# hi and lo of the attention stage's weight tiles from casting and adding DMAs, in a hybrid decoder block

## The chip, the cores and the metric

One core of one Trainium2 chip runs the whole kernel. The metric is the device time of one execution in microseconds; times shown are medians of several runs. The engines are TensorE (PE in the profile, its weight loads PEld), VectorE (DVE), ScalarE (ACT), GpSimd (POOL) and SyncE (SP), which issues DMAs.

## The reference

One decoder layer on 512 tokens of width 1024, in float32. The first half mixes tokens: a combined projection gives queries, three pairs of keys and values, gates, and the inputs of a short convolution.

```python
h = rms_norm(x, norm_mix_pre[l])
u = h @ w_in[l]
q, k_c, v_c, k_s, v_s, k_w, v_w, gl, b_g, c_g, x_t = jnp.split(u, split_points(), axis=-1)
o_nsa = nsa_attention(...)            # compressed, selected and window branch, gated
o_conv = short_conv_mixer(b_g, c_g, x_t, conv_mix_w[l])
y = jnp.concatenate([o_nsa, o_conv], axis=-1) @ w_out[l]
x = x + rms_norm(y, norm_mix_post[l])
h = rms_norm(x, norm_ffn_pre[l])
gu = causal_dwconv(h @ w_ffn_up[l], ffn_conv_w[l])
g, up = jnp.split(gu, 2, axis=-1)
y = (gelu(g) * up) @ w_ffn_down[l]
x = x + rms_norm(y, norm_ffn_post[l])
```

The compressed branch first runs its keys and values, in blocks of 32 tokens, through a small two-layer network (`compress_kv`); its first layer has 2048 x 256 weights for keys and as many for values.

## The kernel before

TensorE multiplies in the type float32r. To keep float32's accuracy every operand is kept as two float32r tiles: hi, the value rounded to 12 significant bits, and lo, the exact rest. A product is three passes, hi x hi, hi x lo and lo x hi (`mm3`, L166 to L169).

The dense weights come as tiles of 128 x 1024 through one `Stream` object, `W`, in the order of their use. `_load` (L68) takes one of three raw buffers and loads 512 KB by a DMA on SP (L72). `_split` (L75) takes one of four buffers of the ring, which holds hi and lo side by side; ScalarE copies the raw tile into hi (L84), and VectorE subtracts hi from the raw tile into lo (L85). For the tiles named in `pool_lo`, the eight of the compression's first layer, GpSimd does the subtraction. `next` hands out a tile and has `ahead` split two and load three more tiles further on.

The tiles in order are: v0 to v2 (values and gates), k0, k1 and c0 (keys of two branches, keys to compress), q0, q1, c1, q2, then with q3 the compression's first layer in eight tiles (`c1_0` to `c1_7`, in the profile `raw_c` and `w_c`) and for each of the four convolution channel tiles a gate g, an input x and an output gate b (`tg`, `tx`, `tb`); after that the output projection's eight (o4 to o7, o0 to o3), 44 of the MLP's first product and 22 of its second.

The start of the kernel, up to L357, runs in the order in which it is written. Behind that a scheduler orders each engine's instructions by their priority and by the time at which it expects their inputs, so TensorE's projection products (`filler`, L535) and the attention's pieces are interleaved. `fill` says how many steps of the projections go between the pieces. The order of the steps is a string: two tiles of the compression are used for one projection tile until all eight are done.

```python
ORDER = ("c1 q2:4 h0 q2:4 h1 q3:4 h2 q3:4 h3 g0:4 h4 g0:4 h5 x0:4 h6 x0:4 h7 s b0 "
         "g1 x1 b1 g2 x2 b2 g3 x3 b3")
```

Here hN is a tile of the compression's first layer (`hidden_steps`, eight products at L441), s its second layer, and a number behind a colon counts steps of three products. The attention goes through four query tiles and two groups of heads in parts. Each part takes logits (L593), adds the bias and finds the row minimum on VectorE (L597), exponentials on ScalarE (L599), scaling by the gate and the sum, for one of four heads on GpSimd (L611) and for three on ScalarE (L613), transposes on TensorE (L622), splits the result into hi and lo (L131, L132) and multiplies it by the values (L630, L631). VectorE also places the values to compress in blocks (L417), and GpSimd takes part in the convolution (L505, L507, L511).

Of the kernel before, what the change touches and what calls it, by code (L numbers as in the profile page):

```python
"""Hybrid decoder block (NSA heads + short convolution, then a gated conv MLP) on one core.

Float32 products run as three float32r passes over operands split exactly into
hi + lo (12 + 12 significant bits): hi*hi + hi*lo + lo*hi.  The attention logits
and the P.V products keep all four parts.

With these shapes N_SEL covers every key block (n_sel = SEQ / L_SLC) and WINDOW =
SEQ, so the selected and the sliding branch both see exactly the causal keys: top-k
only permutes the blocks, and softmax does not depend on their order.
"""  # L10
# [11 lines left out]
F32 = mybir.dt.float32  # L22
# [8 lines left out]
NT = S // P          # token tiles  # L31
KT = D // P          # contraction tiles of the model width
# [9 lines left out]
# the projections and the first layer of the compression as they fill the gaps of the attention:  # L42
# values to compress c1, queries q, hidden layer h, second layer s, then gate g, input x, output gate b
# [3 lines left out]
T_TILES = 20         # kc vc ks kw q0-3 then (c x b) x 4  # L47
WARM = 8             # products on zeros while the first loads are under way


def f32(ap):
    return ap.bitcast(F32)


class Stream:
    """The dense weights in the order of their use: loaded some tiles ahead, split fewer ahead."""

    def __init__(self, tc, nc, raw, ring, items, loads=3, splits=2):
        self.tc, self.nc, self.raw, self.ring, self.items = tc, nc, raw, ring, items
        self.loads, self.splits = loads, splits  # L60
        self.raws, self.tiles = [], []
        self.at = 0
        self.early = False     # whether the splits go before what was emitted shortly before them
        self.pool_lo = set()  # tiles whose lo part GpSimd makes
        self.pieces = {}     # tiles that are split in pieces of so many columns
        self.other = {}      # tiles that go to another pool than the ring

    def _load(self):  # L68
        n = len(self.raws)
        src, cols, name = self.items[n][:3]  # L70
        t = self.raw.tile([P, 1024], F32, tag="raw", name=f"raw_{name}")
        self.nc.sync.dma_start(t[:, :cols], src)  # L72
        self.raws.append(t)

    def _split(self):  # L75
        n = len(self.tiles)
        _, cols, name = self.items[n][:3]
        pool, tag, bufs = self.other.get(name, (self.ring, "ring", None))
        t = pool.tile([P, 2, 1024], F32R, tag=tag, bufs=bufs, name=f"w_{name}")
        eng = self.nc.gpsimd if name in self.pool_lo else self.nc.vector  # L80
        step = self.pieces.get(name, cols)
        for c in range(0, cols, step):
            cs = slice(c, c + step)
            self.nc.scalar.activation(t[:, 0, cs], self.raws[n][:, cs], AF.Copy)  # L84
            eng.tensor_tensor(t[:, 1, cs], self.raws[n][:, cs], f32(t[:, 0, cs]), op=ALU.subtract)  # L85
        self.tiles.append(t)

    def ahead(self, splits, loads):
        last = len(self.items)
        while len(self.tiles) < min(self.at + splits, last):  # L90
            while len(self.raws) <= len(self.tiles):
                self._load()
            with self.tc.high_priority(30) if self.early else nullcontext():
                self._split()
        while len(self.raws) < min(self.at + loads, last):
            self._load()

# [10 lines left out]
def block_kernel(ctx: ExitStack, tc: tile.TileContext, a, out):  # L108
# [20 lines left out]
    def split(hi, lo, src):  # L129
        """hi = src rounded to 12 significant bits, lo = src - hi (exact)."""  # L130
        act(hi, src, AF.Copy)  # L131
        nc.vector.tensor_tensor(lo, src, f32(hi), op=ALU.subtract)  # L132

    VK = [0, 2, 5, KT]       # the k tiles of the value columns, as they share a tile of the ring
# [29 lines left out]
    W.pool_lo |= {f"c1_{c}" for c in range(8)}  # L164
# [28 lines left out]
    # the tensor engine's clock comes up while the first loads are under way  # L193
# [6 lines left out]
    # bias tables: U[p, h, u] = -(bias of distance p + 384 - u), +BIG where it is negative  # L200
    # row r of vrows is the whole of vd; reading with a pitch one short shifts it by r
# [6 lines left out]
    def load(what):  # L208
        """A name of LOADS: w the next weights, g the gains, b and v the bias (its table, then its vector),
        s rows of shifted bias, T columns and x rows of the input."""  # L210
        if what == "w":
            W.ahead(0, len(W.raws) + 1)
        elif what == "g":
            nc.sync.dma_start(gT, a["g_mix_pre"])
        elif what == "b":
            nc.sync.dma_start(oh[:NB, :S], a["onehot"])
            nc.sync.dma_start(relT, a["relT"])
        elif what == "v":
            nc.sync.dma_start(vd[:, :S], vec[:NH, :S])
            nc.sync.dma_start(vd[:, S:], vbig)  # L220
        elif what[0] == "s":
            n = int(what[1])
            nc.sync.dma_start(vrows[n], bass.AP(tensor=vd.tensor, offset=vd.offset + n * 4 * 640,
                                                ap=[[0, P], [1, 4 * 640]]))
        elif what[0] == "T":
            k = int(what[1])
            nc.sync.dma_start(xT[:, k, :], a["xT"][k * P:(k + 1) * P, :])
        else:
            t = int(what[1])
            nc.sync.dma_start(xt[:, t, :], a["x"][t * P:(t + 1) * P, :])  # L230
# [17 lines left out]
    def rstd_of(ss, name):  # L248
        """1 / rms of a row from the two halves of its mean square."""
        r = const.tile([P, 1], F32, tag="rstd", bufs=4, name=name)  # L250
        nc.gpsimd.tensor_scalar(r, ss[:, 0:1], ss[:, 1:2], EPS, op0=ALU.add, op1=ALU.add)  # L251
        nc.gpsimd.tensor_tensor(r, r, mhalf, op=ALU.pow)
        return r
# [17 lines left out]
    # The mean square of a row divides what comes out of the products, not what goes in.  # L271
    R = const.tile([P, 2, NT], F32, name="R")        # 1 / rms and its negative, by token
    Rb = ph1.tile([P, S], F32, name="Rb")            # the same, by token along the row
# [114 lines left out]
    # queries, scaled by -1/8; even heads keep hi in the low half, odd heads in the high half  # L388
# [14 lines left out]
    # X[(l parity, d), l // 2, k/v, hi/lo, (group, block)] = kv + pe, the blocks padded to 32  # L403
# [25 lines left out]
    def hidden_steps(c):  # L429
        """First layer of the compression; rows 0-63 from X hi, rows 64-127 from X lo."""  # L430
# [3 lines left out]
        for l in range(2):  # L434
            l2 = 2 * c + l
            for kv in range(2):
                xs = X[:, l2, kv].rearrange("p s g n -> p (s g n)")
                for s in range(2):
                    cc = slice(l * 512 + kv * 256, l * 512 + kv * 256 + 256)
                    # one group over the bank: its first product opens it  # L440
                    MM(phs[0][:, kv * 256:kv * 256 + 256], xs, w[:, s, cc],  # L441
                       start=l2 == 0 and kv == 0 and s == 0, stop=l2 == 15 and kv == 1 and s == 1)
            yield

    def second_layer():
        w2 = ph1.tile([P, 2, 2, HD], F32, tag="gz", bufs=1, name="w2")     # (half, k/v)
# [127 lines left out]
    class Part:  # L574
        """Four heads of a group on a tile of queries: one branch, or both for the first tile."""
# [76 lines left out]
    def finish(o, i, g):  # L652
        # rows 0-63: V hi . P, rows 64-127: V lo . P
# [23 lines left out]
    for n, (i, g, bs) in enumerate(parts):  # L677
# [6 lines left out]
        # the share that goes between this part's pieces  # L684
# [45 lines left out]
    def token_major(w_tiles, ys, acts, on_half, on_tile, order):  # L730
        """The last products of a streamed contraction, one token tile after another."""
# [14 lines left out]
    with tc.tile_pool(name="ph2", bufs=1, reuse_waits="tile") as ph2:  # L746
# [49 lines left out]
        # the first tiles of the MLP in halves of the tokens, behind the norm of the last rows  # L796
# [83 lines left out]
def _bucket_onehot():  # L880
    """[bucket, 511 - distance], a constant of the shapes alone."""
# [56 lines left out]
```

## Time and profile before

| what | value |
|---|---|
| median of 3 runs | 636.11 us (634.45 to 637.34) |
| span of the profiled execution | 633.9 us |
| its own time | not recorded apart from the span; the median run is 2.2 us longer than that span |
| TensorE, VectorE, ScalarE, GpSimd busy | 97%, 60%, 48%, 10% of the span |
| moved by DMA | 72.00 MB, 114 GB/s on the mean |

A busy share is a mean over the whole span. Matmuls overlap each other in the record: one of 512 columns is shown with 389 ns, yet the next begins some 230 ns behind it, so the distance between starts tells how fast they go. A time line lists instructions by start and duration; what stands in brackets is the engine's idle time just before and what ended it.

### The profile page before, as it was taken

The page shows a single profiled execution, that of the slowest core. Times are in us where ns is not written, and L with a number is a line of the kernel's source. Part 1 is how long each engine was busy: PE and PEld are TensorE (multiplying, and loading weights), DVE is VectorE, ACT ScalarE, POOL GpSimd, SP SyncE. Part 2 cuts the span into 40 slices and gives each one's busy share as a digit, 9 for nine tenths or more (in the row PEclk, how much of TensorE's full clock was granted, in tenths as well). Part 3 has the DMA queues.
Part 4 walks back from the last instruction along what each step waited for, and adds up shares of the span by engine and source line. Part 5 has one row for each costly group of instructions (what it writes and reads, how often), then busy time and mean ns, then how long its engine had stood idle before and what let it go on. Part 6 is the DMA issues. An engine that isn't in the chain of part 4 may idle for free.

```text
span 633.9 us, 8027 instructions
## 1 busy us (share of the span) xinstructions
PE 617.5 (97%) x2980; PEld 511.3 (81%) x2980; DVE 382.2 (60%) x668; ACT 306.5 (48%) x556; POOL 62.7 (10%) x88
## 2 busy tenths in 40 slices
PE   8998899999999999999999999999999999999995
PEld 6886688887778788898888888888888888888884
DVE  5379967898988756648666656565656542222225
ACT  6546765798878644426443434444344422222212
POOL 1102453002130202200000000000000000000001
PEclk9999899999999999999999999999999999999999
DMA  8993355201121483004222233232322232232203
GB/s 293 329 304 129 133 180 189 74 10 43 42 78 53 169 280 130 8 5 143 93 96 98 99 100 101 100 100 99 101 87 95 89 114 87 94 100 99 67 0 133
DMA packets 25302, 72.00 MB, mean 114 GB/s; under 512 B 3136, under 2 KB 7048, under 8 KB 25008
## 3 DMA queue, kind: packets, MB, share of 16 engines
q1 hardware_dynamic: 25264, 71.50, 33.9%
q8 instruction: 23, 0.38, 0.2%
q14 instruction: 15, 0.12, 0.1%
HBM read 67.50 MB, written 4.74 MB: 114 GB/s over the span
## 4 chain that ended last, share of the span: by engine, by line
PE 80%; DVE 10%; DMA 3%; ACT 3%; issue 2%; POOL 1%; SPq 0%; DVEq 0%; POOLq 0%; ACTq 0%
PE pu L168 13%; PE pu L169 13%; PE pu L167 13%; PE z L743 6%; PE z L742 6%; PE z L744 6%; PE y L744 2%; PE y L743 2%; PE y L742 2%; DVE x L417 2%; DMA raw_q<-in_w_t 2%; PE tr L622 2%; PE sc L593 2%; PE o L631 1%; PE o L630 1%
## 5 line engine op out<-in xcount | busy, mean ns | idle before, releaser
L167 PE MATMUL pu<-h2T,w_u 128*128 128x512 f32 (+1 forms) x384 | 142.8, 372 | 0.0
L168 PE MATMUL pu<-h2T,w_u 128*128 128x512 f32 (+1 forms) x384 | 142.7, 372 | 0.0
L169 PE MATMUL pu<-h2T,w_u 128*128 128x512 f32 (+1 forms) x384 | 142.6, 371 | 0.0
L167 PEld LDWEIGHTS pu<-h2T,w_u 128*128 128x128 f32 x384 | 72.3, 188 | 12.6
L168 PEld LDWEIGHTS pu<-h2T,w_u 128*128 128x128 f32 x384 | 72.3, 188 | 12.6 <-DVE h2T L132 0.2
L169 PEld LDWEIGHTS pu<-h2T,w_u 128*128 128x128 f32 x384 | 72.3, 188 | 12.4
L826 DVE SCALAR_TENSOR_TENSOR cv<-pu,ffnw,cv 128x511 f32<-128x511 f32 x44 | 32.9, 749 | 70.2 <-ACT cv L825 70.2
L85 DVE TENSOR_TENSOR w_d<-raw_d,w_d 128x1024 fp32r<-128x1024 f32 x22 | 26.9, 1224 | 72.8 <-ACT w_d L84 72.8
L742 PE MATMUL z<-w_d,aT 128*128 128x512 f32 x176 | 68.5, 389 | 0.0
L743 PE MATMUL z<-w_d,aT 128*128 128x512 f32 x176 | 68.5, 389 | 0.0
L744 PE MATMUL z<-w_d,aT 128*128 128x512 f32 x176 | 68.5, 389 | 0.0
L825 ACT ACTIVATE cv<-pu,ffnw 128x512 f32<-128x512 f32 x44 | 30.3, 688 | 64.0 <-PE pu L169 63.9
L84 ACT ACTIVATE w_d<-raw_d 128x1024 fp32r<-128x1024 f32 x22 | 23.3, 1059 | 75.2 <-PE z L744 75.2
L85 DVE TENSOR_TENSOR w_u<-raw_u,w_u 128x1024 fp32r<-128x1024 f32 x44 | 53.4, 1217 | 5.9 <-ACT w_u L84 5.8
L84 ACT ACTIVATE w_u<-raw_u 128x1024 fp32r<-128x1024 f32 x44 | 46.2, 1052 | 6.6 <-PE pu L169 6.3
L599 ACT ACTIVATE P<-P,mins 128x512 f32<-128x512 f32 (+3 forms) x64 | 35.4, 554 | 11.5 <-DVE mins L597 11.1
L742 PEld LDWEIGHTS z<-w_d,aT 128*128 128x128 f32 x176 | 33.0, 188 | 6.9
L744 PEld LDWEIGHTS z<-w_d,aT 128*128 128x128 f32 x176 | 33.0, 188 | 6.9
L743 PEld LDWEIGHTS z<-w_d,aT 128*128 128x128 f32 x176 | 33.0, 188 | 6.7
L131 ACT ACTIVATE aT<-cv 128x512 fp32r<-128x512 f32 x22 | 13.9, 632 | 49.5 <-DVE cv L843 49.5
L251 POOL TENSOR_SCALAR rsz<-ssz 128x1 f32<-128x1 f32 x4 | 1.2, 300 | 355.2 <-ACT jz L865 355.2
L827 DVE SCALAR_TENSOR_TENSOR cv<-pu,ffnw,cv 128x510 f32<-128x510 f32 x44 | 32.8, 748 | 1.5
(215 smaller groups left out, 1158.7 us busy)
## 6 DMA issues: line engine op xcount, KB each, us to landing
raw_u<-in_w_u SPq DMA_DIRECT2D x44, 512.0 KB, 3.3
raw_d<-in_w_d SPq DMA_DIRECT2D x22, 512.0 KB, 3.2
raw_c<-in_w_c SPq DMA_DIRECT2D x8, 512.0 KB, 3.3
raw_o<-in_w_o SPq DMA_DIRECT2D x8, 512.0 KB, 3.4
vrows<-vd SPq DMA_DIRECT2D x2, 1280.0 KB, 10.4
xT<-in_xT SPq DMA_DIRECT2D x8, 256.0 KB, 5.3
xt<-in_x SPq DMA_DIRECT2D x4, 512.0 KB, 7.1
raw_q<-in_w_t SPq DMA_DIRECT2D x4, 512.0 KB, 7.0
```

The lines of the kernel that those rows point to most:

```text
L84: self.nc.scalar.activation(t[:, 0, cs], self.raws[n][:, cs], AF.Copy)
L85: eng.tensor_tensor(t[:, 1, cs], self.raws[n][:, cs], f32(t[:, 0, cs]), op=ALU.subtract)
L167: MM(dst, wh, xh, start=first, stop=False)
L168: MM(dst, wh, xl, start=False, stop=False)
L169: MM(dst, wl, xh, start=False, stop=last)
L599: act(v, v, AF.Exp, bias=m, scale=-1.0, accum_out=self.sums[:, r, b:b + 1])
L742: MM(y, oh_, w[:, 0, cs], start=first, stop=False)
L743: MM(y, ol_, w[:, 0, cs], start=False, stop=False)
L744: MM(y, oh_, w[:, 1, cs], start=False, stop=last)
L825: act(t, pu, AF.Copy, scale=ffnw[:, m, 2:3])
L826: nc.vector.scalar_tensor_tensor(t[:, 1:], pu[:, :S - 1], ffnw[:, m, 1:2], t[:, 1:], op0=ALU.mult, op1=ALU.add)
L827: nc.vector.scalar_tensor_tensor(t[:, 2:], pu[:, :S - 2], ffnw[:, m, 0:1], t[:, 2:], op0=ALU.mult, op1=ALU.add)
```

## The change

A set `direct` names 25 tiles, from q0 to the last output gate (all that lie before o4 in the order and behind c0). For these `_load` takes a ring buffer instead of a raw one and lets GpSimd issue a DMA that casts float32 to float32r into the hi half. `_split` lets ScalarE write -hi into the lo half, and GpSimd issue a second DMA that reads the same weights again and adds them to it, so lo = w - hi. `_full` stops `ahead` from loading such a tile more than two places ahead of the next one to be handed out. `pool_lo` stays empty. Comments and docstrings are removed too, with the line count of most places kept.

```diff
+        self.direct = set()
     def _load(self):
         n = len(self.raws)
         src, cols, name = self.items[n][:3]
+        if name in self.direct:
+            pool, tag, bufs = self.other.get(name, (self.ring, "ring", None))
+            t = pool.tile([P, 2, 1024], F32R, tag=tag, bufs=bufs, name=f"w_{name}")
+            self.nc.gpsimd.dma_start(t[:, 0, :cols], src)
+            self.raws.append(t)
+            return
         t = self.raw.tile([P, 1024], F32, tag="raw", name=f"raw_{name}")
...
     def _split(self):
         n = len(self.tiles)
-        _, cols, name = self.items[n][:3]
+        src, cols, name = self.items[n][:3]
+        if name in self.direct:
+
+            t = self.raws[n]
+            self.nc.scalar.activation(t[:, 1, :cols], f32(t[:, 0, :cols]), AF.Copy, scale=-1.0)
+            self.nc.gpsimd.dma_start(t[:, 1, :cols], src, accum_op=ALU.add)
+            self.tiles.append(t)
+            return
...
-        while len(self.raws) < min(self.at + loads, last):
+        while len(self.raws) < min(self.at + loads, last) and not self._full():
             self._load()
+
+    def _full(self):
+
+        n = len(self.raws)
+        return self.items[n][2] in self.direct and n > self.at + 2
...
-    W.pool_lo |= {f"c1_{c}" for c in range(8)}
+    names = [x[2] for x in items]
+    W.direct |= set(names[names.index("q0"):names.index("o4")])
```

## Rows read from the trace of the kernel before

**Rows 1.** The page, busy time of each engine over the span.
```profile
PE 617.5 (97%) x2980; PEld 511.3 (81%) x2980; DVE 382.2 (60%) x668; ACT 306.5 (48%) x556; POOL 62.7 (10%) x88
```

**Rows 2.** Busy time by stretch; last columns granted clock, DMA share, GB/s.
```profile
20.00:50.00 30.00, 30.00 (x138) 24.76 (x137) 18.00 (x36) 13.71 (x24) 2.25 (x7) 1.00 1.02 307
36.00:60.00 24.00, 22.77 (x98) 17.74 (x96) 23.10 (x47) 13.45 (x24) 1.11 (x1) 1.00 0.72 204
60.00:84.00 24.00, 20.26 (x99) 16.39 (x99) 22.69 (x34) 17.24 (x31) 13.36 (x8) 0.93 0.46 154
84.00:106.00 22.00, 21.82 (x116) 18.58 (x117) 13.74 (x14) 13.00 (x15) 10.89 (x6) 1.00 0.58 191
106.00:220.00 114.00, 111.99 (x600) 89.57 (x600) 96.15 (x299) 91.82 (x239) 20.38 (x29) 1.00 0.20 63
```

**Rows 3.** The chain that ended last, 22 to 62 us: start, duration, what.
```profile
22.99 11.78 DMA raw_q<-in_w_t
...
42.56 1.12 DVE w_q L85
...
45.67 0.58 DVE x L417
...
58.70 1.23 DVE w_q L85
...
61.13 2.10 DVE x L417
```

**Rows 4.** Time line of GpSimd, 58 to 66 us.
```profile
58.89 1.60 POOL L611 TENSOR_SCALAR P<-P,sums 128x512 f32<-128x512 f32 x1 [30.76 <-DVE sums L606]
60.45 4.97 POOL L85 TENSOR_TENSOR w_c<-raw_c,w_c 128x1024 fp32r<-128x1024 f32 x2
```

**Rows 5.** Time line of TensorE, pieces between 57 and 101 us.
```profile
58.91 0.40 PE L167 MATMUL pp_q<-hT,w_q 128*128 128x512 f32 x1
...
60.54 0.33 PE L622 MATMUL tr<-ident,P 128*128 128x128 f32 x1 [0.78 <-POOL P L611]
...
67.60 0.45 PE L622 MATMUL tr<-ident,P 128*128 128x128 f32 x1 [2.96 <-ACT P L613]
...
85.48 0.40 PE L167 MATMUL pcg<-hT,w_tg 128*128 128x512 f32 x1
...
88.23 1.11 PE L441 MATMUL ph<-w_c,X 128*128 128x256 f32 x8
...
91.93 1.11 PE L441 MATMUL ph<-w_c,X 128*128 128x256 f32 x8
92.88 0.40 PE L167 MATMUL pxt<-hT,w_tx 128*128 128x512 f32 x1
...
100.28 0.40 PE L167 MATMUL pbg<-hT,w_tb 128*128 128x512 f32 x1
```

**Rows 6.** Groups of instructions by line and form: busy us, mean ns, idle before.
```profile
L85 POOL TENSOR_TENSOR w_c<-raw_c,w_c 128x1024 fp32r<-128x1024 f32 x8 | 19.6, 2460 | 14.8 <-ACT w_c L84 14.7
...
L84 ACT ACTIVATE w_c<-raw_c 128x1024 fp32r<-128x1024 f32 x10 | 10.6, 1055 | 5.3 <-DMA raw_c<-in_w_t 1.9 <-PE pcg L169 1.6 <-issue 1.6
...
L85 DVE TENSOR_TENSOR w_tg<-raw_tg,w_tg 128x1024 fp32r<-128x1024 f32 x4 | 5.8, 1451 | 1.1 <-ACT w_tg L84 1.1
```

**Rows 7.** DMA issues: count, KB each, median us from issue to landing.
```profile
raw_c<-in_w_c SPq DMA_DIRECT2D x8, 512.0 KB, 3.3
...
U<-vrows SPq DMA_DIRECT2D x2, 1024.0 KB, 8.2
```

**Rows 8.** One tile's instructions: SP's issues, min/median/max ns.
```profile
L72 SPq DMA_DIRECT2D raw_c<-in_w_c x8: 327/328/1001, 44.3 to 88.4; - x8
```

**Rows 9.** The chain that ended last, 106 to 200 us.
```profile
118.42 0.44 PE tr L622 x4
...
143.80 1.96 DVE w_tb L85
...
160.63 2.06 DVE w_tg L85
```

## Prediction, on record before the changed kernel ran

> **What bounds the kernel now.** I read the page's busy shares first, then the stage of the change cut into stretches, then the chain of waits in order of time, and last the time lines of TensorE and GpSimd. The busy shares [rows 1] say TensorE is busy 97% of a span of 633.9 us, VectorE 60%; an average over stages, so it decides nothing yet. The stretches do [rows 2]. From 36 to 84 us VectorE is busy 23.10 of 24 and 22.69 of 24 us, and TensorE misses 1.23 and 3.74 us; from 84 to 106 TensorE is full (21.82 of 22) and VectorE is at 62%; from 106 to 220 both are high, TensorE missing 2.01 of 114. TensorE's idle time from 36 to 220 is thus 1.23 + 3.74 + 0.18 + 2.01 = 7.2 us, and with the granted clock at 0.93 from 60 to 84 (0.07 x 20.3 = 1.4 us) some 8.6 us is the most that a better fed TensorE could win here.
>
> The chain confirms it: from 36 to 61 us it is almost all VectorE, and the splits L85 stand in it (one of six between 35.9 and 81 us is shown at 42.56, another at 58.70) [rows 3]. Beside them L417 shows 0.58 us alone and 2.10 at 61.13, where GpSimd runs two of its own splits (4.97 us from 60.45) [rows 3, 4]: two-input work on the two engines overlaps and VectorE's slows. TensorE's longest gap, 2.96 us ahead of 67.60, ends on ScalarE's scaling, which had waited for VectorE [rows 5]. From 84.76 us on the chain is products: a group of three tiles (a projection tile with two of the compression's) takes 92.88 - 85.48 = 7.4 us of products without a gap, as does the next, to 100.28 [rows 5].
>
> **What goes.** The 25 tiles from q0 to the last output gate lose their subtraction: 17 on VectorE at 1.2 to 1.45 us, 8 on GpSimd at 2.46 (19.6 us) [rows 3, 6]. Of the 17, six stand in the VectorE-bound stretch (about 7.2 us with q0's) and three in the chain after 140 us (1.96 and 2.06 shown, one of 1.21) [rows 3, 9]. L417's extra time under GpSimd's splits goes too (1.52 us in the piece shown, and one more such piece). SP loses 25 issues of 0.33 us or more [rows 8]; SP sets no time here, so nothing. ScalarE keeps one pass per tile: the copy took 1.06 us [rows 6]; a negating copy of the same size I take at the same, half to twice that as bounds, since it also reads SBUF.
>
> **What comes.** Fifty DMAs issued by GpSimd, two per tile, with a dependent chain between them: load, negation on ScalarE, adding load. No DMA of GpSimd's stands in the trace. One issue on SP took 0.33 to 1.0 us [rows 8]; I take 1.0, with 0.3 and 2 as bounds, and fifty of them (50 us over some 190) fill no engine: GpSimd loses 19.6 us and has about 26 left from 36 to 220 [rows 2]. A plain load of 512 KB lands in 3.3 us, and in 11.8 where the queues are full [rows 3, 7]; the adding one reads the tile as well as HBM, so between one plain load (3.3) and one of the bias pieces of 1024 KB (8.2) [rows 7]: I take 5.0. One tile then needs 1.0 + 3.3 + 0.3 + 1.06 + 1.0 + 5.0 = 11.7 us from load to use, with 8.3 and 19 as bounds. Before, the raw buffers hid the load and only the split sat in the ring.
>
> **The ring.** It has four buffers, and now a buffer is held from the load on. Three tiles are in use for 6.5, 0.95 and 0.95 us in a dense group [rows 5], 2.8 on the mean. Four buffers thus give a group of three tiles every 3 x (11.7 + 2.8) / 4 = 10.9 us (8.3 to 16.4). The DMA engines set a second limit: from 84 to 106 us 191 GB/s took a share of 0.58, so 329 GB/s at full share and 1.6 us per 512 KB [rows 2]; a tile costs 1.6 for the load and 1.6 to 3.2 for the adding one, a group 9.6 to 14.4 us, 12 in the middle. The larger counts: 12 us per group. Four groups (q2 to the last compression tile) run now from 58.91 to 100.28, 41.4 us [rows 5]: the first two slow, bound by VectorE (13.3 each), the last two at 7.4. At 12 each they take 48: **+6.6 us**. VectorE's relief is inside this sum: it makes the first two 1.3 shorter each, and the last two lose 4.6 each.
>
> The Trainium skill has a rule that bears on this: its page "Collectives: The Full Stack" (section "The bandwidth ceiling: the fold count and why AG ≠ RS ≠ AR") says an addition in the DMA path is slow not for the adding but for two source reads on one read ring, measured there at about half a copy's rate. No run here shows it. By it the upper end, 14.4 us a group, would hold; it is the third rival below.
>
> **The other terms.** (a) q0, q1 and c1 come while the DMA engines are full: share 1.02 from 20 to 50 us [rows 2]. q0's plain load took 11.8 us there [rows 3], and its adding load stands on GpSimd behind c1's load, which waits for the second key projection. TensorE starts q0 at about 39 us now; I put it at 42, and of the 3 us one is absorbed by the idle time from 36 to 60: **+2** (0 to 6). (b) While tiles are late TensorE can take attention work that is ready: four transposed chunks of the second part at 0.44 plus two products of 0.23 each, and eight logit products, 3.6 + 1.8 = 5.4 us in all [rows 5, 9]; the 0.23 is a twelfth of the 2.75 us from 85.48 to 88.23 [rows 5]. Half of it, **-2.7** (0 to -5.4). (c) After 106 us tiles come every 10 us and the ring is no limit; VectorE's splits leave the chain: the 5.2 us seen are shared with other waits and TensorE misses only 2.0 us there, so **-2** (0 to -5.2). (d) GpSimd now waits: an adding DMA waits for ScalarE's negation, a load for a free buffer. Queued behind it are the scaling of P (L611, sixteen times) and the convolution's steps (L505 to L511); TensorE's transposes wait for the first, as 0.78 us ahead of 60.54 shows [rows 4, 5]. Two of the sixteen hit for about 1 us: **+2** (0 to 6).
>
> Sum: 6.6 + 2 - 2.7 - 2 + 2 = +5.9 us on the profiled span of 633.9, so 639.8; the median of the runs, 636.11, lies 2.2 above that span, so **642 us**.
>
> **The rivals.** *Faster*: VectorE's relief decides, because the adding load is as quick as a plain one and hidden. For it: VectorE's 95% from 36 to 84 and its splits in the chain. Against it: TensorE's idle time is only 7.2 us, and the last two groups have no slack at all. Its point: a group at 9.6 us or less gives 38.4 - 41.4 = -3, and with -2.7 and -2.5 (no GpSimd waits) -8: 628 us. *No change*: groups near 10.5 us, relief and late tiles cancel: 636. *Two reads bind*: 14.4 us a group, 57.6 - 41.4 = +16.2 in place of 6.6: 652. For it: DMA already at 0.58 in the dense stretch with one read per tile. *GpSimd's queue*: each of the sixteen scalings waits 1 us and TensorE with it: +16 in place of 2, 656. Against it: GpSimd is idle 90% of the span [rows 1]. That the change doesn't do what it says is out: the subtractions are gone from the code, and their rows must be too.
>
> **Chances.** About 0.5% (3.2 us) is what a measurement of this kernel tells from no change. Forecast 0.36, two reads 0.10, GpSimd's queue 0.06: slower 0.52. No change 0.24. Faster 0.24. The forecast's own range is 639.5 to 648. For 8 in 10 the range reaches from 629 (nearly the faster rival) to 656 (past the two reads, up to the queue).
>
> **What would show it.** Right: weight loads of projection products wait for a DMA between 60 and 105 us, groups of three tiles step 10 us or more, the last compression tile ends near 107 (100.3 now), VectorE's share from 36 to 84 falls well below 95%, L417 stays at 0.58. Wrong: products stay dense from 84 to 106 and the first logits come earlier. What would upset it most: an order of TensorE's queue that puts much attention work into the gaps, adding loads that land in 3.5 us, or the granted clock falling in the new gaps, as it did to 0.93 from 60 to 84 [rows 2].

## The result: 6.1% slower, with the profile of the changed kernel

The changed kernel takes **674.63 us** (median of 5 runs, 671.72 to 675.21) against 635.49 of the kernel before beside it: a ratio of 1.0607, interval 1.0586 to 1.0629. The direction was the predicted one, the size was not: +39 us where the prediction had +5.9, and outside its range of 629 to 656. The profiled execution's span is 672.8 us, 38.9 above that of before.

From the page of the changed kernel: the span, the busy times, the DMA queues (packets, MB, the time of their packets as a share of the span of all 16 DMA engines; q0 is here GpSimd's queue, not the tile) and the DMA issues (count, KB each, median us from issue to landing).

```profile
span 672.8 us, 8033 instructions
PE 631.5 (94%) x2980; PEld 522.6 (78%) x2980; DVE 354.0 (53%) x651; ACT 307.0 (46%) x556; POOL 75.6 (11%) x130
q1 hardware_dynamic: 21664, 58.39, 26.1%
q0 software_dynamic: 7200, 26.22, 17.1%
w_c<-in_w_c POOLq DMA_DIRECT2D x16, 512.0 KB, 6.0
w_tg<-in_w_t POOLq DMA_DIRECT2D x8, 512.0 KB, 5.4
KK<-KK SPq DMA_DIRECT2D x4, 256.0 KB, 13.0
```

VectorE gave up 28.2 us (382.2 in [rows 1]) and nothing came of it. TensorE did the same 2980 products and was busy 14.0 us longer with them: its granted clock is lower, as the stretches show. The copies of the keys on SP's queue, which the change doesn't touch, land after 13.0 us where they took 6.6.

The stretches that answer to [rows 2]:

```profile
20.00:50.00 30.00, 27.27 (x120) 22.16 (x120) 14.95 (x32) 13.56 (x24) 7.28 (x13) 0.94 1.04 305
36.00:60.00 24.00, 19.64 (x78) 15.21 (x76) 14.45 (x25) 8.50 (x13) 4.57 (x6) 0.93 1.09 265
60.00:84.00 24.00, 16.37 (x69) 13.39 (x70) 12.65 (x29) 12.93 (x24) 5.60 (x8) 0.79 0.64 151
84.00:106.00 22.00, 18.18 (x87) 14.91 (x86) 7.16 (x15) 12.35 (x19) 7.34 (x11) 0.92 0.91 210
106.00:220.00 114.00, 100.05 (x496) 80.25 (x495) 62.69 (x197) 73.00 (x162) 28.79 (x42) 0.91 0.54 121
```

Cuts at fixed times compare different work. The attention stage has marks that both traces share: the first and the last product of the compression's first layer (ph) and the last group of logits (sc). In the kernel before these stand at 60.6, 100.2 and 208.3 us, in the changed one at 76.1, 127.7 and 246.6. The same view cut there, first the kernel before, then the changed one (columns as in [rows 2]: PE, PEld, DVE, ACT, POOL, granted clock, DMA share, GB/s):

```profile
36.00:60.60 24.60, 22.83 (x99) 17.80 (x98) 23.70 (x48) 14.05 (x25) 1.71 (x2) 1.00 0.70 199
60.60:100.20 39.60, 36.22 (x188) 30.33 (x189) 31.02 (x41) 25.68 (x40) 20.17 (x10) 0.96 0.52 171
100.20:208.30 108.10, 106.54 (x579) 85.97 (x578) 91.86 (x282) 88.18 (x220) 19.57 (x27) 1.00 0.20 63
```

```profile
36.00:76.10 40.10, 29.99 (x111) 23.46 (x110) 20.48 (x40) 16.64 (x28) 8.18 (x11) 0.83 0.86 214
76.10:127.70 51.60, 38.46 (x180) 31.75 (x179) 16.40 (x33) 21.38 (x31) 17.40 (x25) 0.89 0.92 205
127.70:246.60 118.90, 111.53 (x576) 89.87 (x576) 80.00 (x272) 89.93 (x221) 26.93 (x41) 0.95 0.42 97
```

The reader is to see three things. The loss has three places: the **start** (24.6 to 40.1 us, +15.5), the **groups** (39.6 to 51.6, +12.0) and the part **behind the groups** (108.1 to 118.9, +10.8); their sum is 38.3 of the 38.9 us. Second, in each of them TensorE waits: its idle time is 10.1 + 13.1 + 7.4 = 30.6 us where it was 1.8 + 3.4 + 1.6 = 6.7, which makes 23.9 of the 38.3. Third, the other 14.4 are slower products: 179.98 us busy over 867 products against 165.59 over 866, with the granted clock at 0.83, 0.89 and 0.95 where it was 1.00, 0.96 and 1.00. Busy time multiplied by the granted clock is nearly the same in both kernels, 165.1 and 164.1 us, so the products themselves are no more work. The clock is low behind the gaps (the last section has two such rows), so a gap is paid for twice.

The chain that ended last, where [rows 3] showed VectorE's splits, is now made of the new DMAs (start, duration, what):

```profile
42.76 7.95 issue
50.75 0.50 POOL w_q L89
51.27 11.96 DMA w_c<-in_w_c
63.39 1.06 ACT w_c L88
64.45 0.53 ACT Q L417
65.00 0.70 DVE Q L418
65.74 2.08 PE sc L613 x4
...
80.11 5.84 DMA w_c<-in_w_c
86.04 1.07 ACT w_c L88
87.11 0.30 issue
87.41 6.68 DMA w_c<-in_w_c
94.13 1.10 PE ph L461 x7
...
102.60 7.60 DMA w_c<-in_w_c
...
112.96 5.01 DMA w_c<-in_w_c
...
120.67 8.01 DMA w_tb<-in_w_t
```

At 80.11 one whole tile is to be read: the load 5.84 us, the negation 1.07, GpSimd's wake-up 0.30, the adding DMA 6.68, and the product at 94.13, with the load's own issue (0.53 before 80.11) 14.6 us where the prediction had 11.7. Ahead of it stands the start: a load of 11.96 us, and behind its negation, on ScalarE and VectorE, the queries (L417, L418) and four products of the logits, for which TensorE stood idle 7.38 us. The pieces at 102.60 and 120.67 are adding DMAs, the one at 112.96 a load. TensorE's time line shows the waits (the bracket is the idle time ahead and what ended it). The first two lines are the two gaps of the start, which together are its 10.1 us of idle time; 72.92 is the first product of q2; the last two are late tiles of the compression, whose products stood 3.7 us apart in [rows 5]:

```profile
43.07 0.50 PE L189 MATMUL pp_q<-hT,w_q 128*128 128x512 f32 x1 [2.73 <-DMA w_q<-in_w_t]
...
65.74 2.08 PE L613 MATMUL sc<-KK,Q 128*128 128x512 f32 x4 [7.38 <-DVE Q L418]
...
72.92 0.40 PE L187 MATMUL pp_q<-hT,w_q 128*128 128x512 f32 x1
...
94.13 1.10 PE L461 MATMUL ph<-w_c,X 128*128 128x256 f32 x7 [3.82 <-DMA w_c<-in_w_c]
...
110.25 1.86 PE L461 MATMUL ph<-w_c,X 128*128 128x256 f32 x7 [3.67 <-DMA w_c<-in_w_c]
```

### The profile page after: what moved, and what is told of

It reads as the page before. It is cut to its first block, busy times and chain, and to the rows that moved or that the text cites. A ratio compares the mean times of both kernels' runs of the same rounds, so it can differ in the third digit from the quotient of the medians.

```text
span 672.8 us, 8033 instructions
## 1 busy us (share of the span) xinstructions
PE 631.5 (94%) x2980; PEld 522.6 (78%) x2980; DVE 354.0 (53%) x651; ACT 307.0 (46%) x556; POOL 75.6 (11%) x130
## 4 chain that ended last, share of the span: by engine, by line
PE 78%; DMA 10%; issue 3%; ACT 3%; DVE 2%; POOL 2%; SPq 1%; POOLq 0%; DVEq 0%; ACTq 0%
PE pu L189 12%; PE pu L187 12%; PE pu L188 12%; PE z L764 6%; PE z L763 6%; PE z L762 6%; DMA w_c<-in_w_c 6%; PE y L762 2%; PE y L763 2%; PE y L764 2%; PE sc L613 2%; DMA w_tb<-in_w_t 2%; PE tr L642 1%; PE o L650 1%; PE o L651 1%
## 5 line engine op out<-in xcount | busy, mean ns | idle before, releaser
L613 PE MATMUL sc<-KK,Q 128*128 128x256 f32 (+2 forms) x112 | 30.7, 365 | 7.6 <-DVE Q L418 7.4
```

The costliest lines, as they stand in the source:

```text
L613: MM(sc[:, :n], q, k, start=s == 0, stop=s == 1)
```

## Experiments

Fourteen kernels, all from the changed one. "Start" (from 36 us on), "groups" and "behind" are the three stretches between the marks, for each run from its own trace. Each run is held against the kernel before measured beside it (634.7 to 635.5 us):

| run | what differs | time, us | ratio to before | start | groups | behind |
|---|---|---|---|---|---|---|
| before | | 635.5 | 1 | 24.6 | 39.6 | 108.1 |
| changed | | 674.6 | 1.0607 | 40.1 | 51.6 | 118.9 |
| p1_start | only q0, q1, c1 fed by DMAs | 639.3 | 1.007 [1.0051, 1.0088] | 30.9 | 36.4 | 107.5 |
| p2_dense | only q2 to the first output gate | 659.7 | 1.0378 [1.0346, 1.0410] | 30.1 | 54.7 | 110.9 |
| p3_late | only the last nine tiles | 647.1 | 1.0200 [1.0164, 1.0236] | 23.9 | 39.6 | 117.9 |
| m1_no_add | second DMA overwrites | 655.5 | 1.0313 [1.0260, 1.0365] | 35.7 | 43.9 | 110.8 |
| m7_parallel | two plain loads at once | 638.3 | 1.0044 [1.0015, 1.0073] | 33.5 | 34.5 | 107.9 |
| m2_no_second | no second DMA | 636.1 | 1.0014 [0.9998, 1.0029] | 27.2 | 34.6 | 111.5 |
| m3_neg_pool | negation on GpSimd | 674.9 | 1.0605 [1.0560, 1.0651] | 33.6 | 61.7 | 116.1 |
| m4_o_late | three other loads held back | 672.9 | 1.0595 [1.0577, 1.0613] | 37.7 | 51.1 | 120.8 |
| m5_ring5_raw1 | five ring buffers, one raw | (one run) 703.9 | | 52.0 | 44.9 | 119.1 |
| m5_ring4_raw1 | four ring buffers, one raw | (one run) 708.6 | | 49.0 | 50.1 | 119.1 |
| p3_no_add | p3_late, overwriting | 641.6 | 1.0111 [1.0094, 1.0129] | 25.9 | 39.5 | 114.3 |
| p4_last6 | only the last six tiles | 637.7 | 1.0056 [1.0035, 1.0076] | 24.6 | 39.3 | 110.3 |
| p7_q23 | only q2 and q3 | 637.7 | 1.0049 [1.0035, 1.0062] | 25.2 | 40.6 | 107.6 |
| p5_h8 | only the eight first-layer tiles | 652.0 | 1.0249 [1.0197, 1.0301] | 27.4 | 55.2 | 104.7 |

### Three parts of the change

```diff
-    W.direct |= set(names[names.index("q0"):names.index("o4")])
+    W.direct |= set(names[names.index("q0"):names.index("q2")])    # p1_start
+    W.direct |= set(names[names.index("q2"):names.index("tg1")])   # p2_dense
+    W.direct |= set(names[names.index("tg1"):names.index("o4")])   # p3_late
+    W.pool_lo |= {f"c1_{c}" for c in range(8)} - W.direct
```

> Only q0, q1 and c1 come by casting and adding DMAs, the other 22 tiles as before. Theory of the ring (a tile's two chained transfers hold one of four buffers, so the loss sits where tiles follow each other densely): these three cost about 2 us, 638. Rival of the full DMA engines (six transfers, three of them reading twice, join a stretch whose DMA share is already 1.02): they delay q0, the keys' copies and the bias, 8 to 17 us, 644 to 652. Rival of ScalarE's queue (a negation stands ahead of the queries' split and waits for its load): nothing here, since the load that ScalarE waited 9.8 us for was the first compression tile's; 636.

> Only the 13 tiles from q2 to the first output gate come by casting and adding DMAs. Theory of the ring: most of the loss is here, 20 us or more, 656 or above, with groups of three tiles at 12 to 14 us. Rival of the full DMA engines at the start: the first compression tile's load is then quick (the early six transfers are gone), so only the group time is left, some 10 us, 646. Rival of ScalarE's queue: TensorE's gap behind the first two projections stays as long as that load is late.

> Only the last nine tiles of the attention stage come by casting and adding DMAs. By the prediction's own term they gain 0 to 5 us, 631 to 636, since tiles come every 10 us there and VectorE loses nine splits. Rival: waits of GpSimd and ScalarE for DMAs in order (in the trace after, the stretch behind the second layer of the compression grew by some 11 us) cost 5 to 11 us, 641 to 647.

The three parts cost 4.5, 24.9 and 12.2 us, 41.6 together against 39.1 for the whole: each part loses by itself. p1_start lies nearest the ring's 638; the 644 to 652 of full DMA engines and the 636 of ScalarE's queue didn't come. p2_dense is inside its theory (656 or above) and past the rival's 646; it has the groups' whole loss (54.7 us). For p3_late the prediction's own term failed (631 to 636), and the time is at the upper edge of the rival's 641 to 647. p3_late alone has the loss behind the groups (117.9), with start and groups as before; so what costs there is not handed on from the dense stretch. The start's 15.5 us are not one part's: p1_start lengthens it by 6.3 and p2_dense by 5.5, and p1_start has 3.2 of its 6.3 back in the groups, although it leaves the groups' tiles alone.

### What the second DMA costs: overwriting, parallel, none

```diff
-            self.nc.gpsimd.dma_start(t[:, 1, :cols], src, accum_op=ALU.add)
+            self.nc.gpsimd.dma_start(t[:, 1, :cols], src)      # m1_no_add
```

```diff
             self.nc.gpsimd.dma_start(t[:, 0, :cols], src)
+            self.nc.gpsimd.dma_start(t[:, 1, :cols], src)      # m7_parallel
...
-            self.nc.scalar.activation(t[:, 1, :cols], f32(t[:, 0, :cols]), AF.Copy, scale=-1.0)
-            self.nc.gpsimd.dma_start(t[:, 1, :cols], src, accum_op=ALU.add)
```

> The changed kernel with the second DMA overwriting instead of adding: left out is the addition, so lo holds the weights and not their rest; order, chain and waits stay. Theory of two reads per adding DMA: the second transfer lands in about 3.5 to 4 us instead of 5.4 and the DMA engines are freed, groups of three tiles shrink from 12.9 to 11 us, 655 to 662 in all. Rival, the length of the chain alone: the adding costs little beside the chain's hops, 670 or more.

> The changed kernel with both DMAs issued at the load, side by side, the second a plain casting load too, and no negation: left out are the negation and the addition, so lo holds the weights. The bytes read from HBM stay; the chain of load, ScalarE, second load is gone. Theory of the chain in four buffers: a tile is ready some 6 us after its buffer comes free instead of 12 to 13, groups of three fall to 7.5 to 9 us, 632 to 640. Rival of the DMA engines: two transfers per tile still fill them, 650 or more. Beside the run with the second load that overwrites, the difference is the chain's price.

> The changed kernel without its adding DMAs: each of the 25 tiles has one casting load of hi, and ScalarE writes -hi into the lo part, which is left at that (lo is wrong). The weights are read once, as in the kernel before. First-layer products began at 60.6 us before, at 76.1 us in the changed kernel, at 71.7 with a plain second DMA and at 69.5 with two parallel loads. Theory (the late start is the second DMA's: between 36 and 60 us the 16 DMA engines are full, and the weights' second reading delays the loads and the copies of the keys that TensorE waits for): the first product at 60 to 65 us, groups of three tiles in 8.5 us or less, no loss behind them, the whole at 622 to 633 us. Rival (the ring's buffers and GpSimd's order of issues set the start, whatever the bytes): first product at 68 us or later, 634 to 642 us.

(m2_no_second is the changed kernel with the adding DMA's line alone left out, so it keeps the negation, which m7_parallel leaves out.) The order is 674.6, 655.5, 638.3, 636.1: without the addition 19.1 us come back; with both loads issued at once and no negation between them another 17.2; m2_no_second, with the second reading gone and the negation back, is 2.2 below that. m1_no_add and m7_parallel came inside their theories (655 to 662 and 632 to 640). So the second reading costs little when nobody waits for it; what costs is that it adds and that it stands at the end of a chain.

For the start m2_no_second decides for the first theory: first product at 63.2 us, inside its 60 to 65, so one casting load per tile costs the start 2.6 us; the second DMA brings it to 69.5 (parallel), 71.7 (chained, plain) and 76.1 (adding). For the whole time its theory failed: it expected 622 to 633 us and got 636.1, inside the rival's 634 to 642. The groups do take only 34.6 us, 5.0 less than before, with VectorE busy 15.77 us of 34.60, where it was 31.02 of 39.60. Not all of that is VectorE's relief: p1_start, which changes no tile of the groups, has 36.4 with VectorE busy 26.66; a likely reading is that with a later start some of VectorE's work falls ahead of the mark. The end of the groups, 97.8 us, is 2.4 ahead of the kernel before, and the stretch behind gives back 3.4. Even with a second operand that costs nothing, this supply ends where the kernel before did. Its stretches, to be held against the six rows above:

```profile
36.00:63.20 27.20, 25.21 (x108) 19.70 (x107) 19.88 (x39) 17.05 (x28) 2.90 (x5) 1.00 0.88 243
63.20:97.80 34.60, 32.15 (x179) 27.59 (x179) 15.77 (x32) 21.17 (x31) 6.58 (x13) 1.00 0.50 154
97.80:209.30 111.50, 107.76 (x578) 87.82 (x577) 81.97 (x274) 88.75 (x221) 21.20 (x35) 0.98 0.19 56
```

The queue lines price one DMA, as an estimate. GpSimd's queue in m2_no_second (25 loads) and in m1_no_add (25 loads, 25 plain seconds):

```profile
q0 software_dynamic: 3600, 13.11, 6.7%
w_c<-in_w_c POOLq DMA_DIRECT2D x8, 512.0 KB, 3.6
```

```profile
q0 software_dynamic: 7200, 26.22, 13.2%
w_c<-in_w_c POOLq DMA_DIRECT2D x16, 512.0 KB, 4.7
```

0.067 x 635.2 / 25 = 1.70 us of all 16 engines for a casting load, 0.132 x 652.7 / 50 = 1.72 for one of two; the changed kernel's 0.171 x 672.8 = 115.0 leaves 115.0 - 25 x 1.70 = 72.5 for its 25 adding DMAs, **2.90 us each**, 1.7 times a plain one for the same bytes, if its casting loads cost what they do in m2_no_second. The same sum from p2_dense (13 pairs, 9.2% of 657.2 us) and p3_late (9 pairs, 6.7% of 643.5 us) gives 2.95 and 3.09.

### The engine of the negation, and other loads in the way

```diff
-            self.nc.scalar.activation(t[:, 1, :cols], f32(t[:, 0, :cols]), AF.Copy, scale=-1.0)
+            self.nc.gpsimd.tensor_scalar(t[:, 1, :cols], f32(t[:, 0, :cols]), -1.0, 1.0, op0=ALU.mult, op1=ALU.mult)   # m3_neg_pool
```

```diff
+        if name in ("o4", "o5", "o6"):                         # m4_o_late: these loads wait for a late tile
+            self.nc.vector.tensor_copy(t[:1, :1], f32(self.tiles[-1][:1, 1, :1]))
```

> The changed kernel with the negation on GpSimd instead of ScalarE, the same sum otherwise. Rival of ScalarE's queue (its negation waits for a load, 9.8 us at 53 us, and the queries' split stands behind it): with the wait gone from ScalarE the first logits come 8 us earlier, 660 to 667. Theory of the chain in four buffers: the tiles are as late as before, 672 to 680, a little later since GpSimd's pass is longer than ScalarE's 1.06 us.

> The changed kernel, but the loads of o4, o5 and o6 wait for a small copy of a late tile, so that SP cannot issue them at 50 us, where they are in the changed kernel's trace. Theory of the full DMA engines: the first compression tile's load falls from 12 us to about 6 and the whole by 4 to 6 us, 669 to 671. Theory of the ring: its load is late by its own chain, no change, 674.

Neither moves the time much. With the negation on GpSimd the start is shorter (33.6 us), since the queries on ScalarE no longer stand behind a waiting negation, and the groups are longer (61.7), where loads now stand behind waiting negations in one queue; the time is the same within 0.3 us, inside the chain's 672 to 680. So ScalarE's order is a cause of the late start (6.5 us shorter without it), but moving the negation doesn't shorten the whole. Three early loads of later weights, which come into the full stretch, are worth 1.7 us at most as measured: 672.9 lies between the two theories, and the interval of its ratio overlaps the changed kernel's, so an effect is not shown.

### A fifth ring buffer

```diff
-        return self.items[n][2] in self.direct and n > self.at + 2
+        return self.items[n][2] in self.direct and n > self.at + 3            # m5_ring5_raw1
-    rawp = ctx.enter_context(tc.tile_pool(name="rawp", bufs=3))
-    ringp = ctx.enter_context(tc.tile_pool(name="ringp", bufs=4))
+    rawp = ctx.enter_context(tc.tile_pool(name="rawp", bufs=1))               # both
+    ringp = ctx.enter_context(tc.tile_pool(name="ringp", bufs=5))             # m5_ring5_raw1
```

> The changed kernel with five ring buffers and loads allowed three places ahead; space for it comes from the raw buffers, one instead of three, which slows the start and all tiles behind the attention, so only the stretch of the compression's products counts (51.6 us from its first to its last in the changed kernel, 39.6 before). Theory of the ring: group time falls by a fifth, from 12.9 to about 10.5 us, the stretch to 42 us. Rival of the DMA engines: they are at a share of 0.9 there already, the stretch stays above 49 us.

> The changed kernel with one buffer for unsplit weight tiles in place of three, and the ring of four left: the control of the run with five ring buffers, which had to give up two of those three. Theory (the ring sets the groups' time): from the first to the last first-layer product 50 to 53 us, as in the changed kernel (51.6) and against 44.9 with five buffers; the whole at 705 to 715 us, since the tiles behind the attention stage lose their lead. Rival (the one unsplit buffer itself changed the groups): 45 us here too.

Both lose some 30 us elsewhere, to the single raw buffer, so only the groups are read, from one run each: 50.1 us with four buffers, inside its text's 50 to 53, and 44.9 with five, between the theory's 42 and the rival's 49. So the number of ring buffers is one limit of the groups. By the prediction's own formula with L = 14.6, a group is 3 x (14.6 + 2.8) / 4 = 13.0 us with four buffers and 10.4 with five. Counted as the prediction counts, from q2's first product (at 72.92 us in the changed kernel, 81.87 with four buffers, 84.78 with five) to the last of the compression, four groups take 54.8, 53.2 and 48.1 us, so 13.7, 13.3 and 12.0 each: the fifth buffer brings half of what the formula says. The DMA share of the groups is 0.88 and 0.89 in the two runs, so they don't tell what takes the other half.

### The loss behind the groups

```diff
-            self.nc.gpsimd.dma_start(t[:, 1, :cols], src, accum_op=ALU.add)
+            self.nc.gpsimd.dma_start(t[:, 1, :cols], src)                     # p3_no_add
```

```diff
-    W.direct |= set(names[names.index("tg1"):names.index("o4")])
+    W.direct |= set(names[names.index("tg2"):names.index("o4")])              # p4_last6
```

> Only the last nine tiles of the attention stage (tg1 to tb3) are fed by the DMAs, and their second DMA writes the weights into the lo part instead of adding them, so that lo of these tiles is left wrong; the number of DMAs, negations and waits stays. With the addition these nine tiles cost 12.2 us (647.1 us), of it 9.8 behind the last product of the compression. Theory (each tile's chain of load, negation and adding DMA is some 12.6 us here, and the first late tiles have too little lead): a plain second DMA takes 1.5 to 3 us out of each chain, and most of the loss with it: 636 to 641 us. Rival (it is the number of DMAs issued and waited for in GpSimd's and ScalarE's queues): the time stays at 645 us or above.

> Only the last six tiles of the attention stage (tg2 to tb3) are fed by the casting and adding DMAs. Theory (only the lead counts: the cost in the last nine tiles is that of the first of them, tg1, whose products stand in TensorE's order ahead of the second layer of the compression; the six behind it are ready before TensorE asks for them): 632 to 638 us. Rival (every late tile costs its share, 12.2 us over nine tiles, by small DMAs on the path that get slower): 6 of 9, some 643 us.

(p3_no_add has p3_late's lines besides this one; in p4_last6 GpSimd makes the lo of the first-layer tiles again.) p4_last6 keeps six of the nine late tiles and only 2.9 of their 12.2 us: its theory (632 to 638) holds, the rival's 643 doesn't. So most of the late loss sits in the first three. Which of them has it was not tried apart; the chain of p3_late shows the first, tg1:

```profile
96.68 5.73 DMA w_tg<-in_w_t
...
102.52 1.07 ACT w_tg L78
103.59 0.30 issue
103.88 5.37 DMA w_tg<-in_w_t
...
109.30 0.79 PE pcg L180
...
112.74 0.39 PE pg L466 x4
```

The load could start only when the last group's products freed a ring buffer; 12.6 us later TensorE got its tile, and behind these products in TensorE's order stands the second layer of the compression (pg), which the compressed branch of the attention needs: 112.7 us against 105.4 before and 105.1 in p4_last6. In p3_no_add the second DMA of this tile takes 3.71 us in place of 5.37 and pg comes 9.9 us behind the last first-layer product instead of 13.2 (5.2 before); 5.5 of the 12.2 us come back (641.6 us, just past the upper edge of its theory's 636 to 641): the addition, with its longer issue on GpSimd (a median of 0.89 us against 0.58), is nearly half of it; the rest stays with the chain. The number of GpSimd's issues, the rival there, can't be the whole: it is the same in both. p4_last6's remaining 2.9 us were not followed further.

### Can any part be had alone?

```diff
-    W.direct |= set(names[names.index("q0"):names.index("o4")])
+    W.direct |= {"q2", "q3"}                                                  # p7_q23
+    W.pool_lo |= {f"c1_{c}" for c in range(8)} - W.direct
+    W.direct |= {f"c1_{c}" for c in range(8)}                                 # p5_h8, in place of these two lines
```

> Only the tiles q2 and q3 are fed by the casting and adding DMAs; GpSimd makes the lo of the first-layer tiles as before. In the kernel before these two splits are two of VectorE's long operations in the stretch of groups (2.1 us of it each with the copy). Theory (VectorE and TensorE share the bound there, and two chains that overlap with two ordinary tiles of the ring are hidden): 632 to 635 us. Rival (each group holds one DMA-fed tile in a ring of four, and the group waits for it): 1 to 3 us per such group, 637 to 641 us.

> Only the eight first-layer tiles are fed by the casting and adding DMAs; the two tiles beside each stay with VectorE, and GpSimd makes no lo. Theory (a group holds one chain of some 13 us in a ring of four, two of whose tiles are ordinary; what VectorE gives up, about 1 us a group, is less than what a late chain costs): the groups take 41 to 44 us against 39.6, the whole 637 to 643 us. Rival (VectorE was the bound of the groups, and the chain is hidden by the ordinary tiles): 36 to 38 us for the groups, 630 to 634 us, faster than before.

No part that was tried. p7_q23 is 3.0 us slower (its rival's side), and p5_h8 16.5, more than either text had: its groups take 55.2 us although VectorE works only 22.96 of them. ScalarE's time line in p5_h8 suggests how an ordinary tile in the ring makes it worse:

```profile
77.35 1.06 ACT L88 ACTIVATE w_tg<-raw_tg 128x1024 fp32r<-128x1024 f32 x1 [4.95 <-PE ph L451]
78.32 1.99 ACT L78 ACTIVATE w_c<-w_c 128x1024 fp32r<-128x1024 f32 x2
```

The ordinary tile's copy (L88) waits 4.95 us for a ring buffer that products must free, and the negations of the two tiles behind it (L78) wait with it in ScalarE's queue; their adding DMAs, and the next products, come after that. At 105.97 the same copy waits 10.30 us, with two negations behind it. No run takes this order alone away, so its share of the 16.5 us is not shown. No version here beats the kernel before.

## Why the prediction had the sign and not the size

Between the +5.9 us of the forecast and the 38.9 of the span lie 33.0: 13.5 in the start, 8.1 in the groups (the ring and the attention work in its gaps, +3.9 forecast against +12.0), 10.8 behind them (terms (c) and (d), which the forecast had at nothing together), 0.6 elsewhere. That it is slower came by the predicted mechanism, late tiles in the ring; most of the size came from two places that the sum held for nearly free.

**The bound of the kernel before: right as far as shown.** m2_no_second and m7_parallel, which relieve VectorE (and GpSimd) of the splits without an adding chain, run the groups in 34.6 and 34.5 us instead of 39.6; p1_start's 36.4 says that part of this is not relief.

**The ring (+6.6): the mechanism right, the size half.** Counted from q2's first product, as the prediction counts, the four groups went from 41.3 to 54.8 us, +13.5 (1.5 us of which the marks put into the start), or 13.7 a group where it had 12. The step that failed is the price of the adding DMA, and the prediction has it twice. Its sum uses the larger count, the DMA engines': 1.6 us of all of them for a load and, in the middle of 1.6 to 3.2, 2.4 for the adding one, so 12 a group. By the queue lines it is 1.70 and 2.90, so 13.8. The smaller count, the ring's 10.9, rests on "I take 5.0" for the landing, from a plain load's 3.3 and a bias piece's 8.2. On the chain of the dense stretch the adding DMAs took 6.7 to 8.0 us, and the loads 5.0 to 5.8 instead of 3.3, at a DMA share of 0.92 where [rows 2] had 0.58. With the L of 14.6 that follows, the ring gives 13.0. Both corrected counts come near the 13.7, and the prediction had both inside its own bounds (L up to 19, 14.4 us by the DMA engines) and took the middle. Which of the two limits binds first is not settled.

The adding DMA's 2.90 us of the engines against 1.70 bears on the third rival. It is 1.7 times a plain DMA, while the rule in the Trainium skill's "Collectives: The Full Stack" (section "The bandwidth ceiling: the fold count and why AG ≠ RS ≠ AR") has about two times, for two source reads on one ring; the trace is near it, somewhat below. The rival's 14.4 us per group is nearer to the 13.7 than the forecast's 12, and its 652 us was still too low, since it kept the forecast's other terms.

**Term (a), the start (+2): the largest miss, +15.5.** The step that failed is that it took q0's delay alone, and stopped there. q0 itself came much as foreseen: first product at 39.73 us (38.91 before), and 2.73 us of waiting at 43.07. The other gap, 7.38 us, is the one behind the first compression tile's load, which took 11.96 us and held the queries and logits on ScalarE and VectorE behind its negation; m3_neg_pool, with the negation elsewhere, has a start of 33.6 us instead of 40.1. One casting load per tile would have fitted the term (+2.6 in m2_no_second). The second DMAs of four tiles are issued into this stretch, from 36.46 to 50.72 us: from 36 to 60 us the share goes from 0.72 [rows 2] to 1.09. The key copies, from 6.6 to 13.0 us, belong to the same picture but don't set the time by themselves: in m7_parallel they took 16.7 and the kernel 638.3 us. The prediction read the full share from 20 to 50 us, but charged it to one load.

**Term (b), attention work in the gaps (-2.7): didn't come.** TensorE's idle time in the groups rose from 3.4 to 13.1 us, and it did no more products there than before (180 against 188 between the marks). m3_neg_pool, m1_no_add and the changed kernel all leave gaps there.

**Term (c), behind the groups (-2): wrong in sign, +10.8.** The step that failed is "Tiles come every 10 us and the ring is no limit". It is true on the mean, and nearly so in p4_last6 for the last six. But the first tile behind the groups has no lead: its load waits for a buffer that the last group frees, and TensorE's order puts its products ahead of the second layer. p3_late shows 9.8 us from that place with nothing wrong earlier.

**Term (d), GpSimd's queue (+2): not seen, and the rival at 656 us isn't borne out.** In the changed kernel's view of the transposes, the idle time of TensorE ahead of them is all here (releaser, us, times):

```profile
  DVE ptl L151: 1.3, 2
  ACT P L633: 0.2, 1
```

GpSimd's scaling isn't among the releasers any more, where it had cost 0.78 us [rows 5]: no transpose is seen to wait for it.

**The clock: named, not priced.** The text names "the granted clock falling in the new gaps" among three things that would upset it most, without a price. It did: 14.4 of 38.3 us are longer products, at a clock down to 0.79 from 60 to 84 us. On the mean each microsecond of new gap came with 1.6 of loss here (38.3 / 23.9). What the time would be with the clock held up was not tried. Where the new gaps stay small (m2_no_second: 1.00, 1.00, 0.98) this part vanishes too.

Of the signs that the prediction listed for "right", four came: products wait for DMAs, groups step over 10 us, VectorE's share from 36 to 84 us falls to 56% (14.45 + 12.65 of 48 us), and the placing of values that was L417 takes 0.56 to 0.59 us throughout. The fifth overshot: the last compression product starts at 127.7 us, where 107 was foreseen.

## What to carry to other kernels

Moving work from a busy engine to DMAs replaces a short operation between two buffers by a chain that holds the buffer from its first link; count buffers x time held, per link at the landing times of the stretch where it will run, not of a quiet one. Look for the first tile behind every dense stretch: it has no lead, whatever the mean rate says, and what stands behind it in TensorE's order pays. And price each new gap of TensorE with the lower clock behind it. First try the cheapest ideal (here, the second DMA left out): if even that ends level, making the part that it leaves out cheaper can't win by itself.

## What the runs showed of the hardware

- An adding DMA of 512 KB from HBM onto SBUF takes some 2.9 us of the 16 engines (the estimate above) and, in the changed kernel, 5.0 to 12.9 us to land, with a median of 6.7; a plain casting one 1.70 us, and 3.6 us as a median of the first-layer tiles where only one runs per tile (m2_no_second).
- Issuing costs GpSimd 0.56 us for a casting load and 0.87 us for an adding one; one view of the changed kernel, min/median/max ns and first and last start:

```profile
L75 POOL DMA_DIRECT2D w_c<-in_w_c x8: 555/562/865, 51.3 to 113.0; - x8
L89 POOL DMA_DIRECT2D w_c<-in_w_c x8: 853/872/923, 64.7 to 119.4; - x8
```

- The negation, in place in SBUF, takes 1.06 us on ScalarE, as its copy did [rows 6]. On GpSimd in m3_neg_pool its medians by tile are 1.04 to 1.07 us, the longest 1.68; GpSimd's two-input subtraction took 2.46 in the kernel before [rows 6].
- TensorE came back from its longest gap at a lower clock. Two stretches of the changed kernel, most of the 7.38 us gap and what follows it:

```profile
60.00:66.00 6.00, 0.26 (x1) 0.26 (x2) 0.97 (x2) 2.56 (x4) 1.26 (x2) 0.61 0.34 128
66.00:72.00 6.00, 6.00 (x16) 4.62 (x17) 2.18 (x9) 3.78 (x10) 0.86 (x2) 0.53 0.77 175
```

Busy for all of the second 6.00 us, at a granted 0.53, near the lower of the two levels (1.2 and 2.4 GHz), it did 16 products. Its products of 512 columns from 67.62 to 71.46 us start 0.43 us apart, where they are 0.23 apart from 71.99 us on.
